# One hybrid decoder layer on one core: the residual stream, convolution rows and norm weights loaded and stored with channels on partitions

## The chip, the cores and the metric

One core of a Trainium2 chip. The time is device microseconds of one execution, the median of three runs. The profile shows one execution of its own.

## The reference

```python
xn = rms_norm(x, norm1_g)
aq, ak, av, az, ab, aa, bq, bk, bv, iq, ik, iw, ga, gb = split(xn @ w_in)
conv_out, conv_new = causal_conv(concat([aq, ak, av]), conv0, conv_w)  # width 4, 1536 channels
oa, ssm_new = gated_delta(...)          # mixer A, chunkwise for the prompt, one step for samples
ob = dsa_attend(...)                    # mixer B: indexer, top k keys, attention
mix = sigmoid(ga) * (oa @ w_out_a) + sigmoid(gb) * (ob @ w_out_b)
h = x + mix @ w_o
hn = rms_norm(h, norm2_g)
y = h + square(relu(hn @ w_up)) @ w_down
```

x is a prompt of 1024 tokens and 8 sample tokens, 1024 channels, float32; the hidden size of the MLP is 4096. The layer also returns the new key/value, indexer, state and convolution rows.

## The kernel before

Activations lie with channels on partitions: `hT[j]` is 128 partitions x 8 channel blocks x the tokens of chunk j, float32. There are three token chunks, of 384, 384 and 264 tokens (the last has the samples). A dense product (`dense`, tile `pdn`) runs three matmuls per block of weights and chunk, because weights and activations are split into a rounded half and a remainder: ScalarE makes the first, VectorE or GpSimd the second (`split`). Weights come by `block`: a load, then such a split, two to four blocks ahead.

Python generators emit the instructions, and `Flow.run`, a list scheduler with its own simple costs, chooses which generator comes next. Every engine then runs its instructions in the emitted order. All loads and stores of this case's change stand in SyncE's (SP's) queue; a row there waits for data and for the row eight before it that used the same of eight semaphores.

The program runs in this order. First the norm of x (x is transposed by TensorE, tile `ptx<-ident,xs`) and the projections: `a_chain` (L570) makes the convolution, with the state `stT` and the weights `cw`, other chains the heads, gates and the gated delta rule. Then `rest`: attention by `value_chain` and `logit_chain`; between its products stands `merge_chain` as filler. `mix_a` multiplies the outputs of mixer A by w_out_a and by the gates, and stores them to `gd`. `merge` (L1566) takes a chunk, loads the output of mixer B (`load_b`, tile `ob`), brings x into `hT[j]`, multiplies `ob` by w_out_b, adds the halves into `mix` and multiplies that by w_o, added into `hT`. It runs for chunk 2, then 0, and at the end, when attention is done and other buffers are free (`ev_5`), for chunk 1 (`REST`). `part` takes the squares of `hT` for the second norm; `pn<-ssq,ones` sums them over the partitions. Last the MLP in eight groups of 512 hidden channels (`mlp_chain`): up into `u`, down added into `hT`; in the eighth group the output rows are made by `out`.

x enters `hT` by 18 loads of 512 channels x up to 128 tokens (`xt`), four TensorE transposes each into PSUM (`ptx`), and copies by VectorE and ScalarE in turn:

```python
for m in range(4):
    T.transpose(pt[:, m * P:m * P + n], xt[:n, m * P:(m + 1) * P], ident[:n, :n])
for m in range(4):
    copy("act" if m % 2 else "dve", hT[j][:, 4 * i + m, c0:c0 + n], pt[:, m * P:m * P + n])
```

The output leaves the same way (`pty`, `yt`). In the eighth group the blocks m = 0 to 3 are done for all chunks and `out(chunks, 0)` is emitted; then m = 4 to 7 chunk by chunk with `out([j], 1)` after each.

Of the kernel before, what the change touches and what calls it, by code (L numbers as in the profile page):

```python
# [20 lines left out]
NS = 8  # L21
# [104 lines left out]
def program(ctx, tc, I, O, dbg=None, upto=99):  # L126
# [273 lines left out]
    def mixers():  # L400
# [168 lines left out]

        def a_chain():  # L570
            cur["p"] = pools["A"]
            cwr = w([48, P], "cwr", tag="j2", bufs=5, pool=C)
            dma(cwr, I["conv_w"][0].rearrange("j (t p) -> (j t) p", p=P))
            ptc = pst("ptc", "pt")
            T.transpose(ptc[:, :48], cwr, ident[:48, :48])
            cw = w([P, 4, 12], "cw")
            V.tensor_copy(cw, ptc[:, :48].rearrange("p (j t) -> p j t", j=4))
            stT = w([P, 12, 24], "stT")
            for g3 in range(3):
                scr = w([24, 512], "scr", tag="j2", bufs=5, pool=C)  # L580
                for j in range(3):
                    dma(scr[8 * j:8 * j + 8], I["state_conv"][0, :, j, g3 * 512:(g3 + 1) * 512])
                pt = pst("pst", "pt")
                for q in range(4):
                    T.transpose(pt[:, q * 24:(q + 1) * 24], scr[:, q * P:(q + 1) * P], ident[:24, :24])
                V.tensor_copy(stT[:, 4 * g3:4 * g3 + 4], pt[:, :96].rearrange("p (t x) -> p t x", t=4))
            dma(O["conv_sample"][0, :, 0:2, :], I["state_conv"][0, :, 1:3, :])
            ucol = w([P, 12, NS + 3], "ucol")
            todo, ws = [], {}
            tiles = list(range(4, 8)) + list(range(4)) + list(range(8, 12))  # L590
# [14 lines left out]
            for i, ct in enumerate(tiles):  # L605
# [35 lines left out]
                if i in (4, 8):  # L641
                    flush(0)
                    flow.set(ev_k4 if i == 4 else ev_q4)
            for g3 in range(3):
                pcv = pst("pcv", "pt")
                for q in range(4):
                    T.transpose(pcv[:NS + 3, q * P:(q + 1) * P], ucol[:, 4 * g3 + q, :], ident)
                cvo = w([NS + 3, 512], "cvo", tag="j2", bufs=5, pool=C)
                copy("act", cvo, pcv[:NS + 3])
                dma(O["conv_sample"][0, :, 2, g3 * 512:(g3 + 1) * 512], cvo[:NS])  # L650
                dma(O["conv_prompt"][0, 0, :, g3 * 512:(g3 + 1) * 512], cvo[NS:])
            flow.set(ev_a)
            yield

# [911 lines left out]
    def merge(js, after=None, ev_mix=None):  # L1566

        mix = {}
        for j in js:
            ob = load_b(j)  # L1570
            mix[j] = parts("mix", j)
            for t, c0, n in tokens(j):
                for i in range(2):
                    xt = w([P, 512], "xt", tag="ld", bufs=3, pool=cur["L"])
                    dma(xt[:n], xrows((I["x_sample"], I["x_prompt"]), t)[:, 512 * i:512 * (i + 1)])
                    pt = pst("ptx", "pt")
                    for m in range(4):
                        T.transpose(pt[:, m * P:m * P + n], xt[:n, m * P:(m + 1) * P], ident[:n, :n])
                    for m in range(4):
                        copy("act" if m % 2 else "dve", hT[j][:, 4 * i + m, c0:c0 + n], pt[:, m * P:m * P + n])  # L1580
                yield
            for m in range(8):
                ws = blocks(1)

                def ev(j, c, p):
                    ga, gb = (w([P, CM], f"g{a}", bufs=3)[:, :CN[j]] for a in "ab")
                    dma(ga, gd[m, :, c])
                    dma(gb, gd[8 + m, :, c])
                    V.tensor_tensor(gb, p, gb, OP.mult)
                    V.tensor_tensor(ga, ga, gb, OP.add)  # L1590
                    split(mix[j](0, m), mix[j](1, m), ga, "act", "pool")
                yield from dense(ws, lambda a, k, j: ob[:, a, k], ev, [j])
        if ev_mix:
            flow.set(ev_mix)
        for m in range(8):
            def ev(j, c, p):
                V.tensor_tensor(hT[j][:, m], hT[j][:, m], p, OP.add)
                if after:
                    after(j, m)
            yield from dense(blocks(2), lambda a, k, j: mix[j](a, k), ev, js)  # L1600

    def rest():
# [100 lines left out]
        def pool_chain():  # L1703

            for t in range(8):
                yield ev_at[t]
            yield ev_mix
            st[4].close()
            mid.close()
            cur["p"] = cur["L"] = st[5] = stage("5", pd=5, pt=3)  # L1710
            cur["spare"] = True
            cur["c12"] = [(st[5], 2), (st[5], 2), (M, 2), (M, 2)]
            for j in REST:
                hT[j] = w([P, 8, CN[j]], f"hT{j}")
            for j in chunks:
                ssq[j], rs[j] = w([P, CN[j]], f"ssq{j}"), w([P, CN[j]], f"rs{j}")
                hn[j] = parts(f"hn{j}", j, f"hn{j}", 2)
            n2 = w([8, P], "n2")
            dma(n2, I["norm2_g"][0].rearrange("(t p) -> t p", p=P))
            pt = pst("ptg", "pt")  # L1720
            T.transpose(pt[:, :8], n2, ident[:8, :8])
            cur["g2"] = w([P, 8], "g2")
            V.tensor_copy(cur["g2"], pt[:, :8])
            flow.set(ev_5)
            yield

# [29 lines left out]
        def mlp_chain():  # L1756
            yield ev_h
            cur["p"] = st[5]
            for j in chunks:
                yield ev_n[j]  # L1760
            for g in range(8):
                u = {j: chunk(f"u{j}", j) for j in chunks}
                for f in range(4):
                    def ev(j, c, p):
                        r = w([P, CM], "r", tag="sq", bufs=3)[:, :CN[j]]
                        V.scalar_tensor_tensor(r, p, 0.0, rs[j], op0=OP.max, op1=OP.mult)
                        S.activation(r, r, AF.Square)
                        split(u[j][:, 0, f], u[j][:, 1, f], r, "act", "pool")
                    yield from dense(blocks(2), lambda a, k, j: hn[j](a, k), ev, chunks)

                def down(m, js):
                    def ev(j, c, p):
                        V.tensor_tensor(hT[j][:, m], hT[j][:, m], p, OP.add)
                    return dense(wd[m], lambda a, k, j: u[j][:, a, k], ev, js)

                wd = {}
                for m in range(8 if g < 7 else 4):
                    wd[m] = blocks(1)
                    yield from down(m, chunks)
            yield from out(chunks, 0)  # L1780
            for m in range(4, 8):
                wd[m] = blocks(1)
            for j in chunks:
                for m in range(4, 8):
                    yield from down(m, [j])
                yield from out([j], 1)

        def out(js, i):
            for j in js:
                for t, c0, n in tokens(j):  # L1790
                    yt = w([P, 512], "yt", tag="ld", bufs=3, pool=cur["L"])
                    pt = pst("pty", "pt")
                    for m in range(4):
                        T.transpose(pt[:n, m * P:(m + 1) * P], hT[j][:, 4 * i + m, c0:c0 + n], ident)
                    copy("act" if i else "dve", yt[:n], pt[:n])
                    dma(xrows((O["y_sample"], O["y_prompt"]), t)[:, 512 * i:512 * (i + 1)], yt[:n])
                    yield

        flow.run([value_chain(), logit_chain(), pool_chain(), merge_chain(), norm_chain(), mlp_chain()], cur)
        st[5].close()  # L1800
# [16 lines left out]
def halves(a):  # L1817
# [1 line left out]


_INS = ['x_prompt', 'x_sample', 'cache_kv', 'cache_kidx', 'page_table', 'state_ssm', 'state_conv',
        'norm1_g', 'conv_w', 'a_log', 'dt_bias', 'gdn_norm_g', 'norm2_g']
_OUTS = [('y_prompt', (1, 1024, 1024)), ('y_sample', (8, 1, 1024)), ('kv_prompt', (1, 1, 1024, 2, 2, 64)),
         ('kidx_prompt', (1, 1, 1024, 64)), ('ssm_prompt', (1, 1, 4, 128, 128)), ('conv_prompt', (1, 1, 3, 1536)),
         ('kv_sample', (1, 8, 1, 2, 2, 64)), ('kidx_sample', (1, 8, 1, 64)), ('ssm_sample', (1, 8, 4, 128, 128)),
         ('conv_sample', (1, 8, 3, 1536))]


def rope_table():
# [14 lines left out]
def arrays_of(inputs):  # L1844
    a = {n: inputs[n] for n in _INS}
    a["rope"] = rope_table()
    gq, gk = np.asarray(inputs["q_norm_g"]), np.asarray(inputs["k_norm_g"])
    a["qk_g"] = np.concatenate([gq, np.roll(gq, 32, 1), gk, np.roll(gk, 32, 1)], 1)
    w = np.asarray(inputs["w_in"])[0]
    wb = np.asarray(inputs["w_out_b"]).reshape(1, 2, 4, 64, D).swapaxes(1, 2).reshape(1, 512, D)  # L1850
    a["w_un"] = tiles(np.concatenate([w[:, C_AQ:C_AB], w[:, C_GA:]], 1), P)
# [4 lines left out]
        a[n] = tiles(np.asarray(k)[0], P)  # L1856
    a["w_dn"] = np.asarray(inputs["w_down"])[0].reshape(8, 4, P, 8, P).transpose(0, 3, 2, 1, 4)
    return {"in_" + n: np.ascontiguousarray(x) for n, x in a.items()}


def build(arrays, dbg=None, upto=99):
# [17 lines left out]
```

## Time and profile before

| | |
|---|---|
| time, median of 3 (lowest to highest) | 1876.12 us (1874.29 to 1876.82) |
| the profiled execution | 1872.74 us; span 1870.9 us |
| TensorE busy | 1790.5 us, 96% |
| VectorE, ScalarE, GpSimd busy | 58%, 44%, 33% |
| mean granted TensorE clock | 0.987 |
| DMA | 199.30 MB, mean 107 GB/s |

The span is from the first to the last instruction; the execution's time has 1.8 us more around it. PE is the time of TensorE's matmuls, PEld of its weight loads, which overlap. Every operation of the engines is recorded by one helper (line L83), so instructions are told apart by their tiles.

### The profile page before, as it was taken

What the parts mean: (1) busy time and instruction counts of PE and PEld (TensorE: products, weight loads), DVE (VectorE), ACT (ScalarE), POOL (GpSimd) and SP (SyncE); (2) the same over time, 40 slices, a digit from 0 to 9 for tenths busy, and PEclk for the clock granted to TensorE, in tenths of its full rate; (3) what the DMA queues carried; (4) which work ended last, traced back from release to release, by engine and by line L of the source; (5) the groups of instructions that cost most, each with busy time, mean ns of one, the idle gap of its engine ahead of it and who ended that gap; (6) DMA issues with size and microseconds to landing.
All of it is one profiled execution on the core that took longest, in us unless ns stands there. A gap on an engine that the chain in (4) does not pass through costs nothing.

```text
span 1870.9 us, 32909 instructions
## 1 busy us (share of the span) xinstructions
PE 1790.5 (96%) x11966; PEld 1715.5 (92%) x11966; DVE 1091.9 (58%) x2956; ACT 830.3 (44%) x1917; POOL 613.8 (33%) x765
## 2 busy tenths in 40 slices
PE   6999988899999999999899889999999999999998
PEld 4899978799898999989789889999999999999998
DVE  7868767998988896177778785323232323232323
ACT  4456684566687532256657544121313131313131
POOL 2434235613422362221443655121312131313130
PEclk9999999999999999999899999999999999999999
DMA  5325464225445444554654452111111111111112
GB/s 174 129 94 178 130 213 121 84 66 151 121 133 149 136 145 120 186 166 122 205 167 148 133 169 79 52 50 47 46 46 46 52 45 51 47 46 46 46 35 91
DMA packets 167764, 199.30 MB, mean 107 GB/s; under 512 B 29521, under 2 KB 112769, under 8 KB 167594
## 3 DMA queue, kind: packets, MB, share of 16 engines
q1 hardware_dynamic: 163314, 183.57, 32.4%
q0 software_dynamic: 4288, 13.64, 2.5%
q8 instruction: 94, 1.54, 0.3%
q14 instruction: 68, 0.56, 0.1%
HBM read 149.51 MB, written 47.73 MB: 105 GB/s over the span
## 4 chain that ended last, share of the span: by engine, by line
PE 45%; DMA 2%; DVE 2%; POOL 1%; issue 1%; ACT 0%; SPq 0%; ACTq 0%; POOLq 0%; DVEq 0%
PE pdn L83 42%; PE po L83 1%; PE ptp L83 1%; PE pat L83 1%; PE pty L83 0%; POOL wc L83 0%; DMA wc28r<-in_w_o 0%; DMA wc64r<-in_w_o 0%; DVE rs L83 0%; DVE wc L83 0%; DMA ld<-obd 0%; PE ptx L83 0%; DVE ga L83 0%; POOL ssq L83 0%; DMA wc58r<-in_w_b 0%
## 5 line engine op out<-in xcount | busy, mean ns | idle before, releaser
L83 PE MATMUL pdn<-u,wc 128*128 128x384 f32 (+1 forms) x2304 | 367.4, 320 | 0.0
L83 PEld LDWEIGHTS pdn<-u,wc 128*128 128x128 f32 x2304 | 362.8, 188 | 0.1
L83 PE MATMUL pdn<-hn,wc 128*128 128x384 f32 (+1 forms) x2304 | 362.1, 319 | 0.0
L83 PEld LDWEIGHTS pdn<-hn,wc 128*128 128x128 f32 x2304 | 360.5, 188 | 0.3
L83 DVE TENSOR_TENSOR hT<-hT,pdn 128x384 f32<-128x384 f32 (+1 forms) x216 | 110.5, 512 | 247.5 <-PE pdn L83 244.4
L83 PE MATMUL pdn<-xn,wu 128*128 128x384 f32 (+1 forms) x1440 | 250.8, 325 | 0.9 <-ACT z L83 0.9
L83 PEld LDWEIGHTS pdn<-xn,wu 128*128 128x128 f32 x1440 | 224.7, 189 | 9.1 <-issue 4.6
L83 DVE SCALAR_TENSOR_TENSOR r<-pdn,rs 128x384 f32<-128x384 f32 (+1 forms) x96 | 49.4, 515 | 273.6 <-PE pdn L83 273.5
L83 POOL TENSOR_TENSOR u<-r,u 128x384 fp32r<-128x384 f32 (+1 forms) x96 | 89.3, 931 | 274.1 <-ACT u L83 247.5
L83 PE MATMUL pa<-xn,wu 128*128 128x384 f32 (+1 forms) x864 | 160.2, 331 | 0.8 <-ACT a L83 0.8
L83 PEld LDWEIGHTS pa<-xn,wu 128*128 128x128 f32 x864 | 141.9, 195 | 3.2 <-ACT a L83 1.1
L83 ACT ACTIVATE r<-r 128x384 f32<-128x384 f32 (+1 forms) x96 | 47.1, 492 | 172.3 <-DVE r L83 171.6
L83 ACT ACTIVATE jka<-sc,nf 128x512 bf16<-128x512 f32 (+3 forms) x124 | 101.4, 822 | 27.0 <-DVE nf L83 21.5
L83 PE MATMUL pdn<-mix,wc 128*128 128x384 f32 (+1 forms) x576 | 100.6, 328 | 4.5 <-DVE wc L83 2.2
L83 PEld LDWEIGHTS pdn<-mix,wc 128*128 128x128 f32 x576 | 94.5, 194 | 7.8 <-ACT mix L83 2.6
L83 DVE SCALAR_TENSOR_TENSOR a<-u,cw,a 128x384 f32<-128x384 f32 (+1 forms) x108 | 76.0, 706 | 9.1 <-ACT a L83 8.1
L83 POOL TENSOR_TENSOR wu<-wu_4r,wu 128x512 fp32r<-128x512 f32 x32 | 42.2, 1318 | 92.6 <-ACT wu L83 77.7
L83 DVE TENSOR_SCALAR_CACHE_REDUCE jk<-sc,cf 128x768 bf16<-128x768 f32 (+1 forms) x62 | 66.1, 1072 | 1.8 <-ACT jka L83 1.7
L83 PE MATMUL pdn<-ob,wc 128*128 128x384 f32 (+1 forms) x288 | 54.7, 337 | 9.1 <-ACT ob L83 4.7
L83 PE MATMUL pqb<-wbq,xn 128*128 128x256 f32 (+1 forms) x432 | 59.1, 286 | 0.0
L83 ACT ACTIVATE lg<-lg,st 128x1024 f32<-128x1024 f32 (+7 forms) x64 | 49.3, 772 | 21.1 <-DVE st L83 19.7
L83 PEld LDWEIGHTS pdn<-ob,wc 128*128 128x128 f32 x288 | 46.9, 196 | 11.9 <-ACT ob L83 5.4
(905 smaller groups left out, 3284.0 us busy)
## 6 DMA issues: line engine op xcount, KB each, us to landing
wu_0r<-in_w_un SPq DMA_DIRECT2D x32, 256.0 KB
wu_4r<-in_w_un SPq DMA_DIRECT2D x32, 256.0 KB
gd<-g SPq DMA_DIRECT2D x32, 192.0 KB
ga<-gd SPq DMA_DIRECT2D x32, 192.0 KB
cqd<-a SPq DMA_DIRECT2D x24, 192.0 KB
xt<-in_x_prompt SPq DMA_DIRECT2D x8, 512.0 KB
obd<-rb SPq DMA_DIRECT2D x16, 256.0 KB
xt<-in_x_prompt SPq DMA_DIRECT2D x16, 256.0 KB
```

Of the source, the lines that this page charges most:

```text
L83: return f(*a, **k)
```

## The change

The host gives x, the convolution weights and state and norm2_g with channels on partitions, and takes the output and the new convolution rows so (this host work is outside of the time). In the kernel:

```diff
 def a_chain():
-    cwr = w([48, P], "cwr", tag="j2", bufs=5, pool=C)
-    dma(cwr, I["conv_w"][0].rearrange("j (t p) -> (j t) p", p=P))
-    ptc = pst("ptc", "pt")
-    T.transpose(ptc[:, :48], cwr, ident[:48, :48])
     cw = w([P, 4, 12], "cw")
-    V.tensor_copy(cw, ptc[:, :48].rearrange("p (j t) -> p j t", j=4))
+    dma(cw, I["conv_wT"])
     stT = w([P, 12, 24], "stT")
-    for g3 in range(3):
-        scr = w([24, 512], "scr", tag="j2", bufs=5, pool=C)
-        for j in range(3):
-            dma(scr[8 * j:8 * j + 8], I["state_conv"][0, :, j, g3 * 512:(g3 + 1) * 512])
-        pt = pst("pst", "pt")
-        for q in range(4):
-            T.transpose(pt[:, q * 24:(q + 1) * 24], scr[:, q * P:(q + 1) * P], ident[:24, :24])
-        V.tensor_copy(stT[:, 4 * g3:4 * g3 + 4], pt[:, :96].rearrange("p (t x) -> p t x", t=4))
+    dma(stT, I["stT"])
...
-    for g3 in range(3):
-        pcv = pst("pcv", "pt")
-        for q in range(4):
-            T.transpose(pcv[:NS + 3, q * P:(q + 1) * P], ucol[:, 4 * g3 + q, :], ident)
-        cvo = w([NS + 3, 512], "cvo", tag="j2", bufs=5, pool=C)
-        copy("act", cvo, pcv[:NS + 3])
-        dma(O["conv_sample"][0, :, 2, g3 * 512:(g3 + 1) * 512], cvo[:NS])
-        dma(O["conv_prompt"][0, 0, :, g3 * 512:(g3 + 1) * 512], cvo[NS:])
+    dma(O["conv_new"], ucol)
 def merge(js, after=None, ev_mix=None):
     for j in js:
         ob = load_b(j)
-        for t, c0, n in tokens(j):
-            for i in range(2):
-                xt = w([P, 512], "xt", tag="ld", bufs=3, pool=cur["L"])
-                dma(xt[:n], xrows((I["x_sample"], I["x_prompt"]), t)[:, 512 * i:512 * (i + 1)])
-                pt = pst("ptx", "pt")
...
-            yield
+        dma(hT[j], I[f"xT{j}"])
+        yield
 # pool_chain: norm2_g
-    dma(n2, I["norm2_g"][0].rearrange("(t p) -> t p", p=P))
-    T.transpose(pt[:, :8], n2, ident[:8, :8])
-    V.tensor_copy(cur["g2"], pt[:, :8])
+    dma(cur["g2"], I["norm2_gT"])
 # mlp_chain, group g
-    for m in range(8 if g < 7 else 4):
-        wd[m] = blocks(1)
-        yield from down(m, chunks)
-yield from out(chunks, 0)
-for j in chunks:
-    for m in range(4, 8):
-        yield from down(m, [j])
-    yield from out([j], 1)
+    for m in range(8):
+        def ev(j, c, p):
+            V.tensor_tensor(hT[j][:, m], hT[j][:, m], p, OP.add)
+            if g == 7:
+                dma(O["yT"][:, m, c], hT[j][:, m])
+        yield from dense(blocks(1), lambda a, k, j: u[j][:, a, k], ev, chunks)
```

The change moves rows on every engine. The first place is SP's queue at the start of the attention stage, where the gates (`gd`, `ga`, `gb`), the query rows (`q`) and the weights of w_out_a (`wc5r`) are loaded. Before, with the semaphores that a row waits for:

```order
L1551 DMA ga<-gd 128x384 [waits DMAHW0_49]
L1551 DMA ga<-gd 128x384 [waits DMAHW1_49]
L1588 DMA gb<-gd 128x264 [waits DMAHW2_49]
L344 DMA gt<-in_qk_g 128x256 [waits DMAHW3_49,PE_49]
L1629 DMA q_10488<-qd 128x256 [waits DMAHW4_49]
L330 DMA rt<-in_rope 128x128 [waits DMAHW5_49]
L1527 DMA ld<-oad_89 128x2x264 [waits DMAHW6_49,DVE_49,Pool_49]
```

And in the changed kernel:

```order
L1533 DMA ga<-gd 128x384 [waits DMAHW4_49]
L1554 DMA hT_11426<-in_xT 128x2112 [waits DMAHW5_49]
L344 DMA gt<-in_qk_g 128x256 [waits DMAHW6_49,PE_49]
L1603 DMA q_10429<-qd 128x256 [waits DMAHW7_49]
L330 DMA rt<-in_rope 128x128 [waits DMAHW0_49]
L1509 DMA ld<-oad_89 128x2x264 [waits DMAHW1_49,DVE_49,Pool_49]
L1535 DMA gd<-ga 128x384 [waits DMAHW2_49,DVE_49]
L1603 DMA q_10608<-qd 128x256 [waits DMAHW3_49]
L213 DMA wc5r<-in_w_a 128x512 [waits DMAHW4_49,DVE_49]
L213 DMA wc6r<-in_w_a 128x512 [waits DMAHW5_49,Pool_49]
```

The x of chunk 2 (`in_xT`, into `hT_11426`) now stands behind the first gate rows; before, its first `xt` load stood 94 rows behind the `gt` row, at the first merge. Row `wc6r` is eight rows behind it and waits for the same semaphore. Chunk 0's load of 128x3072 follows 21 rows later, and chunk 1's at the beginning of the last stage.

The second place is TensorE's queue at the products of `ob` and w_out_b (`wc`) for chunk 1, with `ptx` the transposes of x and `pn` the sums of squares of the chunks 2 and 0. Before, the piece from the third x tile:

```order
L83 MATMUL ptx<-ident,xt 128x128 x4
L83 MATMUL pdn<-ob,wc_13957 128x384 x2
L83 MATMUL pdn<-ob,wc_13988 128x384 x2
L83 MATMUL pdn<-ob,wc_13993 128x384 x2
L83 MATMUL ptx<-ident,xt 128x128 x12
L83 MATMUL pdn<-ob,wc_14144 128x384 x2
...
L83 MATMUL pn<-ssq_13787,ones 128x264
L83 MATMUL pn<-ssq_13791,ones 128x384
```

And in the changed kernel:

```order
L83 MATMUL pdn<-ob,wc_13744 128x384 x2
L83 MATMUL pdn<-ob,wc_13785 128x384 x2
L83 MATMUL pdn<-ob,wc_13790 128x384 x3
L83 MATMUL pn<-ssq_13670,ones 128x264
L83 MATMUL pdn<-ob,wc_13871 128x384 x12
L83 MATMUL pn<-ssq_13674,ones 128x384
L83 MATMUL pdn<-ob,wc_13907 128x384 x12
```

The 24 transposes are gone, and the two `pn` stand behind 35 and 47 of the block's 96 products instead of behind 64. Further up in this queue, more attention products now stand ahead of and among the first products of `ob` for chunk 2, and attention ends earlier among those of chunk 0.

The third place is the end of TensorE's queue: `u` and `wc` are the down product's, `pty` the transposes of the output. Before:

```order
L83 MATMUL pdn<-u_20188,wc_20850 128x384 x12
L83 MATMUL pty<-ident,hT_12838 128x128 x6
L83 MATMUL pdn<-u_20189,wc_20637 128x384 x5
L83 MATMUL pty<-ident,hT_12838 128x128 x3
L83 MATMUL pdn<-u_20189,wc_20637 128x384 x7
...
L83 MATMUL pdn<-u_20189,wc_20850 128x384 x12
L83 MATMUL pty<-ident,hT_13786 128x128 x12
```

And in the changed kernel:

```order
L83 MATMUL pdn<-u_19930,wc_20482 128x384 x12
L83 MATMUL pdn<-u_19931,wc_20482 128x384 x12
L83 MATMUL pdn<-u_19929,wc_20532 128x264 x12
L83 MATMUL pdn<-u_19930,wc_20532 128x384 x12
L83 MATMUL pdn<-u_19931,wc_20532 128x384 x12
```

The products go back to block by block over the three chunks, and nothing of TensorE's follows the last product; SP's queue ends with 24 stores of `hT` instead of 18 of `yt`.

## Rows read from the trace of the kernel before

**Rows 1.** The page, busy us of each engine (share of the span, instructions).

```profile
PE 1790.5 (96%) x11966; PEld 1715.5 (92%) x11966; DVE 1091.9 (58%) x2956; ACT 830.3 (44%) x1917; POOL 613.8 (33%) x765
```

**Rows 2.** Windows: length, busy PE, PEld, DVE, ACT, POOL; clock, DMA share, GB/s.

```profile
0.00:70.00 70.00, 50.73 (x353) 43.86 (x354) 56.16 (x212) 34.67 (x75) 19.25 (x44) 1.00 0.50 149
70.00:740.00 670.00, 640.86 (x4650) 599.18 (x4648) 551.67 (x1746) 403.34 (x1030) 265.25 (x405) 0.98 0.45 133
...
886.00:910.00 24.00, 16.76 (x94) 14.21 (x93) 14.10 (x43) 10.36 (x32) 10.85 (x13) 0.72 0.63 187
910.00:1044.00 134.00, 128.68 (x860) 118.83 (x859) 107.31 (x273) 91.08 (x212) 51.61 (x51) 0.99 0.54 161
1044.00:1142.00 98.00, 87.90 (x487) 82.70 (x485) 77.58 (x111) 48.65 (x106) 63.18 (x50) 0.98 0.51 157
1142.00:1835.00 693.00, 693.00 (x4417) 693.00 (x4417) 190.41 (x347) 171.17 (x315) 168.46 (x158) 1.00 0.15 46
1835.00:1871.00 36.00, 30.97 (x218) 30.22 (x216) 12.27 (x22) 4.69 (x9) 0.00 (x0) 0.98 0.31 118
```

**Rows 3.** Tiles: count, ns min/median/max, first to last start, shapes.

```profile
L83 PE MATMUL ptx<-ident,xt x72: 201/272/476, 902.3 to 1082.9; 128*128 128x128 f32 x64, 8*128 8x8 f32 x8
...
L83 PE MATMUL pty<-ident,hT x72: 270/272/273, 1835.1 to 1865.7; 128*128 128x128 f32 x64, 128*8 128x128 f32 x8
```

**Rows 4.** Timeline of the tail: start, us, engine, operation [idle before <-releaser].

```profile
1825.49 0.43 DVE L83 TENSOR_TENSOR hT<-hT,pdn 128x264 f32<-128x264 f32 x1
...
1831.14 0.43 DVE L83 TENSOR_TENSOR hT<-hT,pdn 128x264 f32<-128x264 f32 x1 [0.90 <-PE pdn L83]
...
1835.35 0.55 DVE L83 TENSOR_TENSOR hT<-hT,pdn 128x384 f32<-128x384 f32 x1 [1.53 <-PE pdn L83]
...
1864.49 1.47 PE L83 MATMUL pty<-ident,hT 128*128 128x128 f32 x12
...
1865.83 1.57 ACT L83 ACTIVATE yt<-pty 128x512 f32<-128x512 f32 x3 [5.29 <-PE pty L83]
```

**Rows 5.** Waits, 1060 to 1086: engine, tile <- releaser: us, times, longest.

```profile
PE pdn L83 <- ACT wc L83: 2.9, 2, 1.8
...
PE pdn L83 <- ACT ob L83: 1.7, 1, 1.7
...
PE ptx L83 <- DMA xt<-in_x_prompt: 1.0, 2, 0.8
```

**Rows 6.** Windows around the first merges, columns as in rows 2.

```profile
790.00:806.00 16.00, 11.77 (x66) 10.57 (x65) 9.29 (x16) 6.22 (x14) 9.86 (x14) 1.00 0.88 261
798.00:802.00 4.00, 3.23 (x17) 2.91 (x18) 2.68 (x6) 0.74 (x2) 3.09 (x6) 1.00 0.97 315
893.00:907.00 14.00, 8.79 (x35) 7.48 (x36) 5.40 (x16) 4.22 (x13) 6.62 (x7) 0.51 0.71 216
```

**Rows 7.** Timeline, PE in 886 to 910.

```profile
897.30 0.59 PE L83 MATMUL pdn<-ob,wc 128*128 128x264 f32 x1 [3.07 <-ACT ob L83]
```

**Rows 8.** Timeline, SP and PE in 786 to 812.

```profile
792.91 0.38 SPq L344 DMA_DIRECT2D gt<-in_qk_g  x1
...
795.12 2.35 PE L83 MATMUL pdn<-oa,wc 128*128 128x384 f32 x12 [2.50 <-DVE ga L83]
...
797.10 0.33 SPq L213 DMA_DIRECT2D wc6r<-in_w_a  x1
```

**Rows 9.** Timeline of the start.

```profile
11.07 0.34 PE L83 MATMUL ptc<-ident,cwr 48*128 48x48 f32 x1 [2.87 <-DMA cwr<-in_conv_w]
11.10 0.19 DVE L83 TENSOR_TENSOR xn<-ptx,xn 128x32 fp32r<-128x32 f32 x1 [2.15 <-ACT xn L83]
...
14.36 1.06 ACT L83 ACTIVATE xs<-xt 128x1024 f32<-128x1024 f32 x1 [3.21 <-DMA xt<-in_x_prompt]
```

**Rows 10.** Timeline of the last merge, first products and last add of squares.

```profile
1068.74 1.57 PE L83 MATMUL pdn<-ob,wc 128*128 128x384 f32 x8
...
1073.74 2.39 POOL L83 TENSOR_TENSOR ssq<-ssq,sq 128x384 f32<-128x384 f32 x2
```

More of the change, by code (lines that the diff above doesn't have):

```diff
@@ L571, in a_chain @@
             cur["p"] = pools["A"]
-            cwr = w([48, P], "cwr", tag="j2", bufs=5, pool=C)
-            dma(cwr, I["conv_w"][0].rearrange("j (t p) -> (j t) p", p=P))
-            ptc = pst("ptc", "pt")
-            T.transpose(ptc[:, :48], cwr, ident[:48, :48])
             cw = w([P, 4, 12], "cw")
-            V.tensor_copy(cw, ptc[:, :48].rearrange("p (j t) -> p j t", j=4))
+            dma(cw, I["conv_wT"])
             stT = w([P, 12, 24], "stT")
-            for g3 in range(3):
-                scr = w([24, 512], "scr", tag="j2", bufs=5, pool=C)
-                for j in range(3):
-                    dma(scr[8 * j:8 * j + 8], I["state_conv"][0, :, j, g3 * 512:(g3 + 1) * 512])
-                pt = pst("pst", "pt")
-                for q in range(4):
-                    T.transpose(pt[:, q * 24:(q + 1) * 24], scr[:, q * P:(q + 1) * P], ident[:24, :24])
-                V.tensor_copy(stT[:, 4 * g3:4 * g3 + 4], pt[:, :96].rearrange("p (t x) -> p t x", t=4))
-            dma(O["conv_sample"][0, :, 0:2, :], I["state_conv"][0, :, 1:3, :])
+            dma(stT, I["stT"])
+            dma(O["conv_old"], I["state_conv"][0, :, 1:3, :])
             ucol = w([P, 12, NS + 3], "ucol")
@@ L1571, in merge @@
             mix[j] = parts("mix", j)
-            for t, c0, n in tokens(j):
-                for i in range(2):
-                    xt = w([P, 512], "xt", tag="ld", bufs=3, pool=cur["L"])
-                    dma(xt[:n], xrows((I["x_sample"], I["x_prompt"]), t)[:, 512 * i:512 * (i + 1)])
-                    pt = pst("ptx", "pt")
[L1577 to L1580, printed above, removed]
-                yield
+            dma(hT[j], I[f"xT{j}"])
+            yield
             for m in range(8):
@@ L1717, in pool_chain @@
                 hn[j] = parts(f"hn{j}", j, f"hn{j}", 2)
-            n2 = w([8, P], "n2")
-            dma(n2, I["norm2_g"][0].rearrange("(t p) -> t p", p=P))
-            pt = pst("ptg", "pt")
-            T.transpose(pt[:, :8], n2, ident[:8, :8])
             cur["g2"] = w([P, 8], "g2")
-            V.tensor_copy(cur["g2"], pt[:, :8])
+            dma(cur["g2"], I["norm2_gT"])
             flow.set(ev_5)
@@ L1769, in mlp_chain @@
                     yield from dense(blocks(2), lambda a, k, j: hn[j](a, k), ev, chunks)
-                def down(m, js):
+                for m in range(8):
                     def ev(j, c, p):
                         V.tensor_tensor(hT[j][:, m], hT[j][:, m], p, OP.add)
-                    return dense(wd[m], lambda a, k, j: u[j][:, a, k], ev, js)
-                wd = {}
-                for m in range(8 if g < 7 else 4):
-                    wd[m] = blocks(1)
-                    yield from down(m, chunks)
-            yield from out(chunks, 0)
-            for m in range(4, 8):
-                wd[m] = blocks(1)
-            for j in chunks:
-                for m in range(4, 8):
-                    yield from down(m, [j])
-                yield from out([j], 1)
[L1788 to L1797, printed above, removed]
+                        if g == 7:
+                            dma(O["yT"][:, m, c], hT[j][:, m])
+                    yield from dense(blocks(1), lambda a, k, j: u[j][:, a, k], ev, chunks)
         flow.run([value_chain(), logit_chain(), pool_chain(), merge_chain(), norm_chain(), mlp_chain()], cur)
@@ L1821 @@
 _INS = ['x_prompt', 'x_sample', 'cache_kv', 'cache_kidx', 'page_table', 'state_ssm', 'state_conv',
-        'norm1_g', 'conv_w', 'a_log', 'dt_bias', 'gdn_norm_g', 'norm2_g']
-_OUTS = [('y_prompt', (1, 1024, 1024)), ('y_sample', (8, 1, 1024)), ('kv_prompt', (1, 1, 1024, 2, 2, 64)),
-         ('kidx_prompt', (1, 1, 1024, 64)), ('ssm_prompt', (1, 1, 4, 128, 128)), ('conv_prompt', (1, 1, 3, 1536)),
+        'norm1_g', 'a_log', 'dt_bias', 'gdn_norm_g']
+_OUTS = [('yT', (128, 8, 1032)), ('kv_prompt', (1, 1, 1024, 2, 2, 64)),
+         ('kidx_prompt', (1, 1, 1024, 64)), ('ssm_prompt', (1, 1, 4, 128, 128)), ('conv_new', (128, 12, 11)),
          ('kv_sample', (1, 8, 1, 2, 2, 64)), ('kidx_sample', (1, 8, 1, 64)), ('ssm_sample', (1, 8, 4, 128, 128)),
-         ('conv_sample', (1, 8, 3, 1536))]
+         ('conv_old', (8, 2, 1536))]
 def rope_table():
@@ L1848, in arrays_of @@
     a["qk_g"] = np.concatenate([gq, np.roll(gq, 32, 1), gk, np.roll(gk, 32, 1)], 1)
+    x = np.concatenate([np.asarray(inputs["x_prompt"])[0], np.asarray(inputs["x_sample"])[:, 0]])
+    for j, (c, n) in enumerate(zip(C0, CN)):
+        a[f"xT{j}"] = x[c:c + n].reshape(n, KT, P).transpose(2, 1, 0)
+    a["conv_wT"] = np.asarray(inputs["conv_w"])[0].reshape(4, 12, P).transpose(2, 0, 1)
+    a["stT"] = np.asarray(inputs["state_conv"])[0].reshape(NS, 3, 12, P).transpose(3, 2, 1, 0).reshape(P, 12, 24)
+    a["norm2_gT"] = np.asarray(inputs["norm2_g"])[0].reshape(8, P).T
     w = np.asarray(inputs["w_in"])[0]
@@ L1858, in arrays_of, with results_of @@
     return {"in_" + n: np.ascontiguousarray(x) for n, x in a.items()}
+def results_of(r):
+    y = r["out_yT"].transpose(2, 1, 0).reshape(NT, D)
+    cv = r["out_conv_new"].transpose(2, 1, 0).reshape(NS + 3, 1536)
+    conv_s = np.concatenate([r["out_conv_old"], cv[:NS, None]], 1)[None]
+    return (y[None, :NP_], y[NP_:, None], r["out_kv_prompt"], r["out_kidx_prompt"], r["out_ssm_prompt"], cv[None, None, NS:],
+            r["out_kv_sample"], r["out_kidx_sample"], r["out_ssm_sample"], conv_s)
 def build(arrays, dbg=None, upto=99):
@@ L1877 @@
     r = run_bass_kernel_spmd(nc, [arrays], core_ids=[0])
-    return tuple(r.results[0]["out_" + n] for n, _ in _OUTS)
+    return results_of(r.results[0])
```

## The prediction

> **What bounds the kernel now.** Four views were read in this order. The page's engine line comes first: TensorE is busy 96% of the span, no other engine above 58% [rows 1]. So a removed instruction pays only if it stood on TensorE, or if TensorE waited for what it fed. The windows by stage come second [rows 2]: the reader is to compare PE's busy column with the length of each stretch. The MLP (1142 to 1835) is busy 693.00 of 693.00, and there TensorE alone decides. The start (0 to 70) leaves 19 us idle, the projection and mixer stage (70 to 740) 29 us, the stretch at 886 to 910 over 7 us at a granted clock of 0.72, the last merge (1044 to 1142) 10 us and the tail 5 us. The tile view comes third, for how many transposes stand where [rows 3], and then the timelines and waits at the places where they stand. The change has six parts. Each is priced against one profiled execution, span 1870.9, 1872.74 as timed; that is 3.4 us under the median of 1876.12, so the forecast is its time less the sum plus 3.4.
>
> **Price of one transpose.** The median of 272 ns in [rows 3] is one transpose's passage and overlaps with its neighbours. The pace is read from a run without gaps: twelve in 1.47 us [rows 4], so (1.47 - 0.27) / 11 = 0.109 us each at full clock.
>
> **Tail (last MLP group).** Now the 72 output transposes stand between matmuls, and after the last one come copies by ScalarE, a store, and the end. In [rows 4] the adds of the short chunk come 1831.14 - 1825.49 = 5.65 us apart, which is one output block over the three chunks. The last add of block 3 ends at 1835.35 + 0.55 = 1835.90. Four blocks more without transposes end at 1835.90 + 4 x 5.65 = 1858.5. In the kernel before the last copy ends at 1865.83 + 1.57 = 1867.40, and the span ends 3.5 us later. I keep 3.5 for the last store, although it has 1,536 bytes a row instead of 2,048: 1862.0 instead of 1870.9, **-8.9**. The terms check: 72 x 0.109 = 7.8, and about 1 for the copy. Twenty-four stores instead of 18 issue one by one beside the matmuls. Bounds: -8 (the last store lands a microsecond later) to -9.5.
>
> **Last merge (REST, chunk 1).** 24 transposes go, 24 x 0.109 = 2.6. TensorE waits here for the x tiles (1.0), for `ob`, whose ScalarE half stands behind the copies out of the transposes (1.7), and for the weights split by ScalarE (2.9) [rows 5]. The first two go with the x path. The weights' wait is partly of the same making, since x loads and weight loads take turns in SP's queue. I take 1.7 of it, the larger half: 2.6 + 1.0 + 1.7 + 1.7 = **-7.0**. Bounds: -2.6, when the weight supply is late anyway, to -11, when nearly all of the stage's 10 us idle but a pipeline's start closes with the transposes. The 1.57 MB load of hT1 now stands among the weights at the head of the stage, ahead of the w_b products; its first taker is the w_o block behind them, 96 products later (96 x 5.65 / 36 is over 15 us).
>
> **First merges (chunks 2 and 0).** 48 transposes, 48 x 0.109 = 5.2. Waits for x tiles cost 1.0 for the 24 of the last merge [rows 5]; for 48 that would be 2.0, and I take 1.3, since filler stands beside them here. From 893 to 907 the granted clock is 0.51, the lower level of 1.2 GHz [rows 6], around a wait of 3.07 us for `ob` [rows 7]; half of the 8.79 us busy there, 4.4, is the price of that. The new order puts more attention products beside that block, so the gap may close, and I give it 1.5: 5.2 + 1.3 + 1.5 = **-8**. Bounds: -3 (part of the transposes filled gaps) to -15 (5.2, 2.0, 4.4 and 3.1 in full).
>
> **The bulk loads in their new place.** hT2 (1.08 MB) and hT0 (1.57 MB) are issued near 793 and 802, where the DMA engines are 0.88 busy over 16 us and 0.97 at 315 GB/s in the middle of it [rows 6]. At 315 GB/s they are 3.4 and 5.0 us of transfer. The gate stream there waits already: TensorE stood 2.50 us for a gate product [rows 8]. Before, the same bytes came in 18 pieces during the merges, where the share is 0.71 or less [rows 2, 6]. So this part costs, and its price is unseen: 0 if the shift of 3.4 and 5.0 is hidden by the filler that TensorE has, 8.4 if it arrives in full. I take half, **+4**.
>
> The Trainium skill's table in DMA: Bandwidth & Descriptors, section Bandwidth, gives 6.15 us for 1 MB, though the same row gives 341 GB/s; by its duration the two would be an estimated 15.5 us instead of 8.4, and half of that would make the sum 3.5 us worse, 1856 or 1857. The trace's 315 GB/s does not show it.
>
> **Start.** Ten loads, 13 transposes and four copies become two loads. TensorE's wait of 2.87 us for the convolution weights is mostly a shadow, since the product behind it takes `xn`, which VectorE finishes at 11.10 + 0.19, 0.2 after the weights' transpose starts [rows 9]. But the second x tile is issued behind part of these loads and taken at 14.36 after a wait of 3.21 [rows 9]; now two loads and a store of state stand ahead of it instead of four loads, which may bring it 1 us sooner, and 12 transposes of the state go (1.3 less what was in gaps). **-2**; bounds 0 (the fill is set by the weights) to -4.
>
> **Convolution rows out.** 12 transposes, 12 x 0.109 = 1.3, in a dense stretch [rows 2]; three ScalarE copies and six stores off the path. **-1.2**; bounds 0 to -1.3. **norm2_g**: one transpose of eight rows becomes one load, needed long after: 0.
>
> The sum is -2 - 1.2 - 8 + 4 - 7 - 8.9 = -23.1. So the profiled execution would take about 1849.6, and the median **1853**.
>
> **Rivals.** B, the bulk loads stop SP's queue. An SP row waits for the row eight before it that uses the same lane, as the order shows: wc6 waits for hT2, and a gate store for hT0. Before, eight issues take 797.10 - 792.91 = 4.2 us [rows 8]. If a load that shares the engines takes 7 to 10 us, all SP work behind it is 3 to 6 us late, twice, at the place where the gates already are late, and what was saved in the first merges is filled with waits: +9 more, **1862**. For it: DMA busy 0.97. Against it: hT2 alone needs 3.4 us, less than 4.2. The Trainium skill says in DMA: Bandwidth & Descriptors, section Queues, rings and completion order, that each engine takes descriptors in ring order; by that the small loads behind a bulk load stand behind all of it, which speaks for B; no row here has so large a load.
>
> C, the waits around the merges go with the transposes and the slow clock with its gap: -15 and -11 in the place of -8 and -7, less a little: **1843**. For it: the copies stand on ScalarE and VectorE in front of `ob` and the weights. Against it: the weights' wait remains.
>
> D, the transposes of x were filler: TensorE waited for weights and gates anyway, only the tail counts, **1867**. Against it: TensorE is busy 128.68 of 134 us from 910 to 1044 [rows 2], where 28 of the 72 stand.
>
> E, slower. The sums of squares of chunks 2 and 0 are now multiplied by `ones` after 35 and 47 products of the last merge, before after 64. TensorE takes its rows in order, so a late sum stops it. One product of 384 columns takes 0.175 us (5.65 us are 12 of 264 columns and 24 of 384, [rows 4]). So the second slot is 47 x 0.175 = 8.2 us after the first product at 1068.74; the last add of squares ended at 1073.74 + 2.39 = 1076.13, 7.4 us after it [rows 10]. The margin is 0.8; each us of lateness beyond it costs one. It decides when this passes the 23 us saved; with 27, **1880**. Against it: GpSimd needs 1.2 us an add [rows 10], the eight adds of a chunk are 10 us, so even sums that start at the first product are 2 us late.
>
> **How the numbers follow.** A change under 0.2%, 3.8 us, can't be told from none here. Chances: the forecast 0.60, B 0.15, C 0.15, D 0.05, E 0.03, and 0.02 for the reordering of the mixer stage, whose rows the scheduler shifts throughout. The likeliest's own range is 1846 to 1860: half of the bulk loads' bounds, and the reordering's few us either way out of 29 idle. 1840 to 1867 takes in B, C and D. Faster than 1872.3: A to D less a little, 0.92; E and part of the rest slower, 0.04; the same, 0.04.
>
> **What would show it.** The span ends 3.5 us after the last add into hT, and 5.65 us lie from block to block to the last; the last merge is some 91 us long instead of 98; no add into hT waits for the bulk loads; around them the DMA share is over 0.9 for longer than 16 us. The forecast is wrong if SP's issue stops after an hT load for more than some 5 us, if TensorE waits at `pn`, if the mixer stage (70 to 740) differs by more than 5 us, or if the gap near 897 grows.

## The result, and the profile after

The changed kernel takes 1850.13 us (median of 4, 1847.85 to 1855.45); before took 1876.29 (median of 4). The ratio is 0.9867, 95% interval 0.9843 to 0.989. Two more measurements of it gave 0.9842 (0.9819 to 0.9864) and 0.9859 (0.9841 to 0.9878): 25 to 30 us faster, where 1853 from 1876 had been forecast.

The profiled execution of it is the slowest of its four (1855.45). Its page, first the span, then the engines' busy time as in [rows 1]:

```profile
span 1853.6 us, 32391 instructions
...
PE 1777.7 (96%) x11796; PEld 1704.4 (92%) x11796; DVE 1087.0 (59%) x2906; ACT 814.3 (44%) x1867; POOL 609.2 (33%) x765
```

TensorE lost 12.8 us of busy time and the span 17.3. The windows, to be held against [rows 2] and [rows 6]:

```profile
0.00:70.00 70.00, 50.56 (x354) 44.33 (x355) 58.52 (x215) 35.23 (x76) 19.15 (x45) 1.00 0.51 156
70.00:740.00 670.00, 640.05 (x4611) 599.29 (x4610) 552.20 (x1716) 397.64 (x1021) 262.78 (x406) 0.97 0.44 130
...
790.00:806.00 16.00, 10.95 (x58) 10.02 (x56) 7.10 (x10) 5.17 (x13) 8.14 (x12) 0.89 0.87 266
893.00:907.00 14.00, 11.68 (x80) 9.92 (x79) 12.44 (x38) 9.53 (x26) 5.81 (x7) 0.98 0.75 213
893.00:917.00 24.00, 20.72 (x123) 17.73 (x122) 20.93 (x58) 16.35 (x44) 10.96 (x14) 0.86 0.59 170
1133.60:1826.00 692.40, 692.40 (x4414) 692.40 (x4413) 190.93 (x347) 171.17 (x315) 168.48 (x158) 1.00 0.16 48
```

The MLP, from 1133.6 on, is as tight as before. In 893 to 907 TensorE is busy 11.68 us instead of 8.79 and the clock 0.98 instead of 0.51, but the hole has not closed: it has moved back and shrunk. The wider window, 893 to 917, shows that, held against the kernel before:

```profile
893.00:917.00 24.00, 18.61 (x116) 16.81 (x117) 12.99 (x41) 11.68 (x37) 11.41 (x13) 0.72 0.69 205
```

The start and the mixer stage look alike in this execution. The tail, to be held against [rows 4]:

```profile
1840.24 0.43 DVE L83 TENSOR_TENSOR hT<-hT,pdn 128x264 f32<-128x264 f32 x1 [0.90 <-PE pdn L83]
...
1845.89 0.43 DVE L83 TENSOR_TENSOR hT<-hT,pdn 128x264 f32<-128x264 f32 x1 [0.90 <-PE pdn L83]
...
1850.10 0.56 DVE L83 TENSOR_TENSOR hT<-hT,pdn 128x384 f32<-128x384 f32 x1 [1.53 <-PE pdn L83]
```

One block every 5.65 us to the very end, and the span ends 1853.6 - 1850.66 = 2.9 us after the last add; 3.5 had been kept for that.

To see where the rest came from, each trace is cut at the same four instructions: the first `pa<-xn` product (end of the start), the first `pdn<-oa` product (first merges begin), the 16th add of `pdn` into hT (chunk 0 done, last merge begins) and the 24th (last merge done). In the kernel before, the last three are these rows of the timeline:

```profile
790.38 2.24 PE L83 MATMUL pdn<-oa,wc 128*128 128x384 f32 x12
...
1070.19 0.54 DVE L83 TENSOR_TENSOR hT<-hT,pdn 128x384 f32<-128x384 f32 x1
...
1135.51 0.55 DVE L83 TENSOR_TENSOR hT<-hT,pdn 128x384 f32<-128x384 f32 x1
```

And in the changed kernel:

```profile
792.47 2.24 PE L83 MATMUL pdn<-oa,wc 128*128 128x384 f32 x12
...
1070.12 0.54 DVE L83 TENSOR_TENSOR hT<-hT,pdn 128x384 f32<-128x384 f32 x1
...
1126.61 0.55 DVE L83 TENSOR_TENSOR hT<-hT,pdn 128x384 f32<-128x384 f32 x1 [2.29 <-PE pdn L83]
```

So the last merge took 1135.51 - 1070.19 = 65.3 us before and 56.5 after; the first merges 279.8 and 277.6. The same cut for every kernel of this study, one profiled execution each, in us:

| kernel | start | mixers | first merges | last merge | MLP and tail | span |
|---|---|---|---|---|---|---|
| before | 107.8 | 682.6 | 279.8 | 65.3 | 735.4 | 1870.9 |
| p1_tail | 109.1 | 681.0 | 280.5 | 64.9 | 726.2 | 1861.7 |
| p2_x | 107.2 | 686.0 | 278.8 | 62.5 | 735.9 | 1870.4 |
| p3_conv | 107.3 | 681.9 | 282.1 | 65.8 | 736.3 | 1873.5 |
| p10_norm_only | 109.7 | 687.9 | 282.3 | 64.1 | 736.3 | 1880.3 |
| p5_x_norm | 106.9 | 687.7 | 277.4 | 54.7 | 736.4 | 1863.2 |
| after | 108.5 | 684.0 | 277.6 | 56.5 | 727.0 | 1853.6 |
| p4_same | 106.2 | 680.1 | 278.6 | 55.0 | 727.0 | 1846.9 |
| p12_same | 106.7 | 678.9 | 277.8 | 54.8 | 727.0 | 1845.2 |
| p6_norm_old | 106.6 | 678.7 | 277.9 | 61.1 | 727.0 | 1851.5 |
| p7_late_first | 105.3 | 677.9 | 279.3 | 54.8 | 727.0 | 1844.3 |
| p8_no_x | 106.8 | 677.6 | 275.8 | 55.4 | 727.2 | 1842.8 |
| p9_norm_early | 106.5 | 681.3 | 278.4 | 61.5 | 732.9 | 1860.6 |
| p11_late_all | 107.6 | 678.9 | 275.7 | 64.4 | 732.9 | 1859.4 |

The same kernel differs by up to 5 us in the mixer stage between its three profiles (678.9 to 684.0), and by 1.0 and 1.7 in the merges; MLP and tail of kernels with the same tail repeat within 1.0, apart from the two at the end.

### The profile page after: what moved, and what is told of

The parts are those of the page before. It is cut to its first block, busy times and chain, and to the rows that moved or that the text cites. A ratio compares the mean times of both kernels' runs of the same rounds, so it can differ in the third digit from the quotient of the medians.

```text
span 1853.6 us, 32391 instructions
## 1 busy us (share of the span) xinstructions
PE 1777.7 (96%) x11796; PEld 1704.4 (92%) x11796; DVE 1087.0 (59%) x2906; ACT 814.3 (44%) x1867; POOL 609.2 (33%) x765
## 5 line engine op out<-in xcount | busy, mean ns | idle before, releaser
L83 PE MATMUL pdn<-u,wc 128*128 128x384 f32 (+1 forms) x2304 | 363.8, 319 | 0.0
L83 DVE SCALAR_TENSOR_TENSOR sc<-rl,wsg,sc 128x512 f32<-128x512 f32 (+1 forms) x70 | 54.4, 781 | 12.2 <-ACT rl L83 12.0
L83 PE MATMUL pdn<-oa,wc 128*128 128x384 f32 (+1 forms) x288 | 53.4, 336 | 6.7 <-DVE ga L83 6.7
L83 PEld LDWEIGHTS pqb<-wbq,xn 128*128 128x128 f32 (+1 forms) x432 | 53.8, 178 | 4.0 <-ACT qx L83 0.8
```

Source lines behind the costliest of these rows:

```text
L83: return f(*a, **k)
```

## The experiments

**One part at a time.** p1_tail is the kernel before with this alone:

```diff
-    yield from out(chunks, 0)
...
+    for m in range(8):
+            if g == 7:
+                dma(O["yT"][:, m, c], hT[j][:, m])
```

> The kernel before with one part of the change: the last MLP group goes block by block and stores hT directly. Theory A (the parts add up and each is worth its own removed TensorE work and waits): 8.9 us less than before, 8 to 9.5, all of it behind the last product of the eighth up projection. Rival D (only the tail counts): this one alone gives nearly the whole 26 us. If the difference is far from 9 us, something upstream is moved by it too.

Measured: ratio 0.9937 (0.9918 to 0.9956), 1864.81 us against 1877.07. That is 12.3 us by the medians and 8 to 15 by the interval. In the traces the MLP and tail take 726.2 instead of 735.4, 9.2 less, and no other stage moves by more than 1.6: it is the forecast term, and D falls.

p2_x changes only the x path:

```diff
-    for t, c0, n in tokens(j):
...
+    dma(hT[j], I[f"xT{j}"])
```

> The kernel before with only the x path changed: one load into hT for each chunk in the place of 18 loads, 72 transposes and 72 copies. Theory A: first merges -8, last merge -7, bulk loads +4, so 11 us less than before. Rival B (the bulk loads stop SP's queue): 2 us less. Rival C (the waits go with the transposes): 20 us less. Rival D: within 3 us of before.

Measured: ratio 0.9974 (0.9962 to 0.9987), 4.9 us, less than half of A's 11. The table says where: the last merge gives 2.8 us where 7 were forecast, and the first merges 1.0 where 4 were. The timeline of the last merge's beginning in p2_x:

```profile
1032.58 0.30 SPq L1711 DMA_DIRECT2D n<-in_norm_g  x1
...
1054.20 0.22 PE L83 MATMUL ptg<-ident,n 8*128 8x8 f32 x1
...
1055.63 0.16 DVE L83 COPY g<-ptg 128x8 f32<-128x8 f32 x1
...
1055.83 5.90 ACT L83 ACTIVATE hn<-hT,g 128x264 fp32r<-128x264 f32 x13 [0.34 <-DVE g L83]
...
1061.34 5.69 DVE L83 SCALAR_TENSOR_TENSOR hn<-hT,g,hn 128x264 fp32r<-128x264 f32 x6
1066.95 1.64 DVE L83 TENSOR_TENSOR ob<-ld,ob 128x384 fp32r<-128x384 f32 x1
...
1068.98 0.68 DVE L83 TENSOR_TENSOR wc<-wc56r,wc 128x512 fp32r<-128x512 f32 x1
...
1069.68 1.23 SPq L1537 DMA_DIRECT2D ld<-obd  x2
1070.96 0.59 SPq L213 DMA_DIRECT2D wc59r<-in_w_b  x1
...
1074.77 0.63 ACT L83 ACTIVATE wc<-wc59r 128x512 fp32r<-128x512 f32 x1 [4.13 <-DMA wc59r<-in_w_b]
...
1075.46 0.62 PE L83 MATMUL pdn<-ob,wc 128*128 128x384 f32 x2 [2.31 <-ACT wc L83]
```

The reader is to follow one chain. norm2_g is asked for at 1032.58, but its transpose (`ptg`) stands in TensorE's queue behind the products of w_o and runs at 1054.20. All scalings by it (`hn`) that had gathered, 13 on ScalarE and 13 on VectorE, then run at once, 5.9 us on the one and, from 1056.4 on, over 10 us on the other. Behind them stand VectorE's half of `ob` (1066.95) and its half of weight wc56 (1068.98). The load of the next `obd` rows waits for VectorE and issues at 1069.68, as the half of wc56 ends (1068.98 + 0.68); and behind that in SP's queue stands weight wc59, for which TensorE waits. The scale, which my sum had at nothing, was the head of the chain.

p3_conv changes only `a_chain` and norm2_g:

```diff
-    dma(cwr, I["conv_w"][0].rearrange("j (t p) -> (j t) p", p=P))
...
+    dma(cw, I["conv_wT"])
+    dma(stT, I["stT"])
...
+    dma(O["conv_new"], ucol)
...
+    dma(cur["g2"], I["norm2_gT"])
```

> The kernel before with only the convolution weights, state, new convolution rows and norm2_g laid out by the host. Theory A: 3.2 us less than before (start 2, convolution rows 1.2), at the edge of what can be told. Rival: the transposes at the start lie in TensorE's idle time there and those in the middle are the only gain, 1.3 us or less. A difference above 6 us either way would mean that the new order of the mixer stage matters more than the removed work.

Measured: ratio 0.9984 (0.9971 to 0.9998), 2.6 us: A's 3.2 within what can be told.

p4_same and, later, p12_same are the changed kernel again, with no edit.

> The changed kernel itself, a second time, for an execution near its median beside the first profiled one, which was 5 us above it. If the difference between its executions comes from TensorE's clock, the two profiles have the same idle time of TensorE by stage and differ in the number of stretches at half clock, 1.7 us for each stretch of 3.4 us. If it comes from transfers, idle time in one stage differs.

> The changed kernel again, on the same chip as the three others, to compare them with: 1847 to 1851.

Measured: 1848.68 and 1849.50. The windows from the start to the first `pdn<-oa`, of the changed kernel's first profile:

```profile
0.00:792.40 792.40, 742.38 (x5310) 695.03 (x5311) 626.30 (x1977) 444.46 (x1128) 292.76 (x463) 0.98 0.45 136
```

and of p4_same:

```profile
0.00:786.20 786.20, 742.02 (x5310) 695.01 (x5311) 625.53 (x1977) 444.11 (x1128) 293.92 (x463) 0.98 0.45 137
```

Same busy time, same clock, 50.0 against 44.2 us idle; the two merges together differ by 0.5. So the difference between these two executions comes from waits in the start and mixer stage, not from the clock: the second half of the expectation holds. What makes those waits differ was not followed.

**What norm2_g is worth.** p5_x_norm is p2_x with one edit more, p10_norm_only is the kernel before with that edit alone, and p6_norm_old is the changed kernel without it:

```diff
-    dma(n2, I["norm2_g"][0].rearrange("(t p) -> t p", p=P))
-    T.transpose(pt[:, :8], n2, ident[:8, :8])
-    V.tensor_copy(cur["g2"], pt[:, :8])
+    dma(cur["g2"], I["norm2_gT"])
```

> The kernel before with the x path and the load of norm2_g changed, convolution and tail as before. The x path alone gave 5 us where I had said 11. Theory F: the load of norm2_g, priced at 0, is what is missing: the scale now comes before ScalarE's idle time at the head of the last stage, so its 16 scalings there no longer stand before the splits of the last merge's weights; with it the two are worth 11 to 13 us. Rival: the missing part comes from the tail or the convolution part, and this kernel stays within 2 us of the x path alone, 5 us below before.

> The changed kernel with only norm2_g loaded and transposed as before. Theory F: 6 to 8 us slower than the changed kernel (1856), all of it between the last attention product and the last product of w_o. Rival: within 2 us of the changed kernel (1849).

> The kernel before with only the load of norm2_g changed. Theory F: within 3 us of before, 1873 to 1876, since attention ends later there and the last stage opens when ScalarE's work is due anyway; the 6 to 7 us of the change come only together with the x path. Rival: the load of norm2_g is worth 6 to 7 us by itself (1869).

Measured: p5_x_norm 1864.27 against 1875.81 (0.9936, 0.9922 to 0.9951), 11.5 us; p6_norm_old 1855.70 (0.9902, 0.9883 to 0.9922), about 6 slower than the changed kernel; p10_norm_only 1880.26 against 1876.76 (1.001, 1.0000 to 1.0021), no gain, if anything a loss of up to 4 us. In the table the last merge is 54.7 us with both edits, 62.5 and 61.1 with the x path alone, 64.1 with norm2_g alone. p6_norm_old has the burst again, just ahead of the last merge:

```profile
1047.07 5.90 ACT L83 ACTIVATE hn<-hT,g 128x264 fp32r<-128x264 f32 x13 [0.35 <-DVE g L83]
```

There it begins 16 us before the last merge (1063.3), in the changed kernel 34 us (1035.7 and 1070.1), under the products of w_o, and the loads of `obd` and the weights follow one another without a stop:

```profile
1032.56 0.33 SPq L1693 DMA_DIRECT2D g<-in_norm_gT  x1
...
1035.69 3.87 ACT L83 ACTIVATE hn<-hT,g 128x264 fp32r<-128x264 f32 x9 [0.47 <-DMA g<-in_norm_gT]
...
1060.28 0.54 SPq L213 DMA_DIRECT2D wc58r<-in_w_b  x1
1061.50 1.23 SPq L1519 DMA_DIRECT2D ld<-obd  x2
1062.78 0.58 SPq L213 DMA_DIRECT2D wc59r<-in_w_b  x1
...
1067.31 0.63 ACT L83 ACTIVATE wc<-wc59r 128x512 fp32r<-128x512 f32 x1 [1.23 <-DMA wc59r<-in_w_b]
```

Its waits in 1050 to 1127 name no weights any more (in [rows 5] they are the largest):

```profile
PE pdn L83 <- ACT mix L83: 3.7, 2, 2.0
PE pdn L83 <- ACT ob L83: 1.4, 1, 1.4
```

Theory F holds for the size and for the need of both edits. Why both are needed can be read from the traces: the scalings begin when the scale is there and the last stage has opened, and that opens after the end of attention. With the old x path attention ends at 1043.5 to 1050.3. There p3_conv and p10_norm_only, which load the scale as the changed kernel does, begin the scalings 24.3 and 26.1 us ahead of the last merge, and it takes 65.8 and 64.1 us. With both edits attention ends at 1020.4 to 1030.7, the scalings begin 33.6 to 35.2 us ahead, and the last merge takes 54.7 to 56.5 us (p9_norm_early and p11_late_all, below, left out). p9_norm_early was to show that the time of arrival counts, by another way: the old transpose, but far ahead.

```diff
 def merge_chain():
     cur["p"] = M
+    n2 = w([8, P], "n2")
+    dma(n2, I["norm2_g"][0].rearrange("(t p) -> t p", p=P))
+    pt = pst("ptg", "pt")
+    T.transpose(pt[:, :8], n2, ident[:8, :8])
+    cur["g2"] = w([P, 8], "g2")
+    V.tensor_copy(cur["g2"], pt[:, :8])
     yield from mix_a()
```

> The changed kernel with norm2_g loaded by rows and transposed by TensorE as before, but ahead of the products of w_out_a, some 250 us before its first use. Theory F says that what counts is when the scale arrives and not how it is laid out: no difference from the changed kernel (1849). Rival: the transpose and the copy themselves, or the layout, make the difference of 6 to 7 us; then this one takes 1855.

Measured: 1862.91 (0.9922, 0.9901 to 0.9944), as neither side said. It doesn't decide whether the layout matters. The scheduler put the end of attention among later products, 1039.6 instead of 1023.6 in p12_same, so the last stage opened later. The scale had been transposed at 790, and still the scalings began only at 1042.7, 23.5 us ahead of the last merge, which took 61.5 us, as with the x path alone. So an early scale is not enough; a short last merge goes with early scalings. The MLP and tail took 5.9 us more, which nothing in the edit's purpose explains (below). That the moment of the scalings is the cause rests on the traces of p2_x, p6_norm_old and after; p9_norm_early only fits it, since its order differs in other places too.

**What the bulk loads cost.** p7_late_first holds the loads of hT2 and hT0 back, p8_no_x leaves the residual out (x isn't loaded, the first w_o product is copied into hT):

```diff
 # p7_late_first
+    if j in FIRST:
+        V.tensor_copy(hT[j][:, 0, :1], ob[:, 0, 0, :1].bitcast(F32))
     dma(hT[j], I[f"xT{j}"])
 # p8_no_x
-    dma(hT[j], I[f"xT{j}"])
...
-    V.tensor_tensor(hT[j][:, m], hT[j][:, m], p, OP.add)
+    V.tensor_copy(hT[j][:, m], p)
```

> The changed kernel with the loads of x for the first two merges held back until the chunk's ob is there (one copy of one column into hT by VectorE orders them). Theory A priced the early loads at 4 us: with them out of the stretch around 790 to 806, the products of w_out_a wait 4 us instead of 8 for the gates, and the kernel is some 4 us faster (1845). Rival: the wait moves to other loads or the loads are late for the first add of w_o; then it is the same or slower than the changed kernel (1849 or more).

> The changed kernel without the residual: x isn't loaded into hT, and the first product of w_o is copied there, not added. It bounds what the bulk loads cost in all places. Theory A: 4 us faster than the changed kernel, as the loads at 790 to 806 cost 4 and hT1's nothing. Rival B in its strong form: 10 us faster or more. Rival: no difference, the loads are hidden.

Measured: p7 1846.12 (0.9846, 0.9821 to 0.987), p8 1844.59 (0.9833, 0.982 to 0.9847), against 1848.7 to 1850.1 for the changed kernel. The place is the one forecast. In p4_same TensorE waits for the gate products, 783 to 822:

```profile
PE pdn L83 <- DVE ga L83: 8.2, 5, 4.0
```

In p8_no_x, 784 to 810, the wait is what it was in the kernel before (4.2):

```profile
PE pdn L83 <- DVE ga L83: 4.2, 4, 2.5
```

The same five waits are 6.7 and 6.1 in the two other profiles of the changed kernel, and 5.9 to 8.2 in the six kernels with early loads (p9 left out); in the seven others they are 4.2. So the loads add 1.7 to 4.0 there, 2.6 on the mean. But it is partly given back: the later wait for `ob` at the first products of w_out_b, 3.07 us in [rows 7], is 0.8 in p4_same, but still 1.2 in p7_late_first and 2.5 in p8_no_x, where the gates came sooner. Over the first merges p8_no_x is 2.2 us under the mean of the six kernels (278.0); with late loads they take 279.3 (p7) and 275.7 (p11), one above that mean and one below. So the net cost of some 2 us is an estimate from one profile of p8_no_x, beside a scatter of 1.0; and p7's lead over the changed kernel, within the intervals, isn't from the merges.

p11_late_all holds all three loads back and loads g2 ahead, to try a version that beats the changed kernel:

```diff
 def merge_chain():
     cur["p"] = M
+    cur["g2"] = w([P, 8], "g2")
+    dma(cur["g2"], I["norm2_gT"])
     yield from mix_a()
...
 def merge(js, after=None, ev_mix=None):
+    V.tensor_copy(hT[j][:, 0, :1], ob[:, 0, 0, :1].bitcast(F32))
     dma(hT[j], I[f"xT{j}"])
```

> A version that might beat the changed kernel: all three loads of x into hT wait for the chunk's ob, and norm2_g's scale is loaded ahead of the products of w_out_a. With the early loads worth 3 us at most, as the kernel without the residual shows, and hT1's load out of the weights' way at the head of the last stage: 1845 to 1847. Rival: the wait for ob and the weights stays, and it is no faster than the changed kernel on this chip.

Measured: 1859.71 (0.9901, 0.9887 to 0.9914), 10 us slower than the changed kernel on the same chip. Its timeline shows rival B in the open, at the last merge:

```profile
1057.22 0.42 SPq L1555 DMA_DIRECT2D hT<-in_xT  x1
...
1059.12 1.68 SPq L213 DMA_DIRECT2D wc59r<-in_w_b  x1
...
1069.70 0.63 ACT L83 ACTIVATE wc<-wc59r 128x512 fp32r<-128x512 f32 x1 [5.91 <-DMA wc59r<-in_w_b]
...
1070.39 2.78 PE L83 MATMUL pdn<-ob,wc 128*128 128x384 f32 x7 [5.94 <-ACT wc L83]
```

256 KB of weights, issued behind the 1.57 MB of x and two loads of `obd` rows, are there only at 1069.6, some 10 us after their issue, and TensorE stands 5.94 us. Each load reports its landing in sixteen parts: those of x come in from 1063.40 to 1067.74, those of the weights from 1066.30 to 1069.62. The Trainium skill says in DMA: Bandwidth & Descriptors, section Queues, rings and completion order, that a DMA engine takes its descriptors in ring order; by that the weights wait on each engine for its part of x, and the trace agrees with that in the order of landing. Another 5.9 us of the loss are again in the MLP and tail.

## Why the prediction was right

The total and its sign were right, and by the tail for the reason given; the other terms were not all right: the x path's part of the last merge was put 3.8 us too high and norm2_g 6.6 us too low. That these two partly cancel in the total is luck. The means are over the kernels of the table that have the part and those that don't.

- **Tail**, forecast -8.9: 736.1 (five kernels) to 726.9 (six, without p8, p9 and p11), **-9.2**.
- **Last merge**, forecast -7 by the x path and 0 by norm2_g: the x path alone 65.0 to 61.8, **-3.2**, near the bound of -2.6 that had been kept for a late weight supply; with norm2_g 55.2, **-9.8**. The step that failed is "one transpose of eight rows becomes one load, needed long after: 0". It was priced by its own length and by its taker's date in the program; its place in TensorE's queue, behind the products of w_o, and what gathered behind it on ScalarE and VectorE weren't looked at. The waits of [rows 5] for `ob` and the weights did have one making, but as p2_x and p5_x_norm show together, a good part of it was this burst and not the x path.
- **First merges and bulk loads**, forecast -8 + 4 = -4: 281.2 (four kernels with the old x path) to 278.0, **-3.2**. If the loads cost 2.2 net, as estimated above, the removal was worth 5.4, about the 48 transposes themselves (5.2). The hole at 897 shrank, but TensorE was held up more at 795 to 810 (in these two profiles the clock is 0.89 in 790 to 806, before 1.00): a part of the waits only moved. The gate wait was forecast in its place and, at 2.6 on the mean (4.0 in one profile), nearly in its size. That it cost less in the end fits that it took over idle time which stood later.
- **Start and convolution rows**, forecast -3.2: -1.3 in the start (108.1 to 106.8) and -5.1 in the mixers (685.0 to 679.9), means of five and nine kernels that scatter by 6 to 7; timed alone, 2.6 with norm2_g, which by itself gave nothing. Of the 6.4, TensorE's busy time accounts for 3.2 (24 transposes of 0.109 are 2.6) and its idle time for 3.2 (49.8 to 46.6). The first was the forecast; whether the second is the new order's or the scatter's stays open. The prediction had named 5 us in this stage as a sign of being wrong, and the mixers lie at that edge.
- **Rivals.** B's mechanism is real, as p11_late_all shows, but in the changed kernel it stays small: wc6 issues 7.0 us behind hT2 in p4_same (788.26 to 795.24) where eight issues took 4.2 [rows 8], and the gate waits grow by 2.6, not by 9. As foretold, no add into hT waits for a load of x. C's number for the last merge (-11) was near, by another cause. E did not come: `pn` follows the products without a wait.

```profile
1074.14 0.61 PE L83 MATMUL pn<-ssq,ones 128*128 128x264 f32 x2
```

The parts add up only if norm2_g is counted with x: p5_x_norm 11.5, p1_tail 12.3 and p3_conv 2.6 make 26.4, each known to some 3 us, against the 26 to 28 measured.

## What to carry to other kernels

The price of a small instruction is not its length but its place: a transpose of 0.2 us in the queue of the bounding engine can hold back a whole burst of other engines' work until that work collides with the next stage. Before pricing an edit at zero, look in the trace for what starts the moment its result is there. The two early bulk loads cost some 2 us by the estimate above, since part of TensorE's waits only moved; the third, held back "until needed", cost 5.9 us, since it then stood just ahead of the next weights.

## What was not expected of the hardware

p9_norm_early and p11_late_all have the same MLP instructions as the changed kernel, yet their MLP and tail take 732.9 us instead of 727.0, all of it at full clock and without waits. The page of p9_norm_early gives for the up products:

```profile
L83 PE MATMUL pdn<-hn,wc 128*128 128x384 f32 (+1 forms) x2304 | 365.8, 320 | 0.0
```

and that of the changed kernel:

```profile
L83 PE MATMUL pdn<-hn,wc 128*128 128x384 f32 (+1 forms) x2304 | 362.1, 319 | 0.0
```

So the up products run 3.7 us longer, with the same count, and the down products 2.1 (365.9 against 363.8); p11_late_all shows the same two figures as p9_norm_early. Together that is 5.8 of the 5.9. What both kernels share is a new tile of 8 floats a partition in the pool of `mix` and hT ahead of the others, which shifts the addresses of what comes after it in memory. That the addresses are the cause was only argued: no run padded that tile.
